# Norms of q and k by one square and one sum by head, and the transposed q and k evicted by one engine

## The chip, the cores and the metric

The kernel runs on one core of a Trainium2 chip. Its time is device time in microseconds (us). The engines are TensorE (PE in the profile's rows, with its weight loads as PEld), VectorE (DVE), ScalarE (ACT), GpSimd (POOL) and SyncE (SP), which issues most DMAs. Each works through its own queue in order and waits for the others by semaphores. Before the change the kernel took 1407.88 us, the median of three runs (1403.77 to 1408.54).

## The reference, cut to what matters

One layer of a decoder is computed for a prompt of 1024 tokens and for 8 sample sequences of 8 tokens, 1088 tokens in all. The part that the change touches is the projection with its norms by head:

```python
def rms_norm(x, w):
    x32 = x.astype(F32)
    y = x32 * lax.rsqrt(jnp.mean(jnp.square(x32), axis=-1, keepdims=True) + EPS)
    return y.astype(x.dtype) * w

p = jnp.einsum('btd,de->bte', rms_norm(x, ln1), w_in)
a, q, k, v, g_a, g_b = jnp.split(p, IN_SPLITS, axis=-1)
heads = lambda t: t.reshape(B, T, N_HEADS, HEAD_DIM)      # 12 heads of 64
return a, rms_norm(heads(q), q_norm), rms_norm(heads(k), k_norm), heads(v), g_a, g_b
```

The 12 heads are three groups of four, with window and dilation (128, 1), (512, 4) and (2048, 16). Each group's attention is computed, the three are combined by their softmax denominators, and then come gates, an output projection and an MLP of width 4096. Everything is float32, and the normed k and v are outputs too.

## The kernel before, in words

**Matmuls.** Each operand of a large matmul is split into a high and a low part (`split`, L115: ScalarE writes the rounded copy, L116, VectorE the difference, L117), and three matmuls (`PASSES`) give one product. TensorE's order is the order of the program (`manual_schedule`). The orders of the other engines' queues are laid down at build time by the framework from a simulated timeline (`schedule_with_timeline_sim`); `behind_pe` ties an instruction to the last matmul issued, so that it isn't sorted ahead of it.

**Stages.** First comes the pooling input (to about 63 us), then the three head groups in the order 2, 1, 0 (to about 416 us), then gates, output projection and MLP, which is over two thirds of the time.

**A head group.** It has nine blocks of tokens: eight of 128 prompt tokens and block 8 with the 64 sample tokens. For blocks 1 to 5 q and k come out of one product (`js = (0, 1)`, 512 columns, a full PSUM bank) and v of another; for blocks 8, 0, 6 and 7 q, k and v are three products of 256 columns. Each product is a call of `qkv_part` (L605). It orders its parts by the place that their weights hold (`js = sorted(js, key=lambda j: wts[j])`, L613), and the three places are handed out in turn.

After a product with q or k, `qkv_part` does the norm:
- squares (L642): for each head one ScalarE activation over 64 columns, from PSUM into the tile qk, with the sum of the squares accumulated into one column of `ms`;
- GpSimd adds the epsilon term (L645) and raises to the power -1/2 (L646) into `r`;
- `scale()` (L648 to L656), put off to the next `step()`, writes qk: for each head one ScalarE copy over 64 columns with `r` as the scale (L651). For the sample block VectorE multiplies k by its norm weights afterwards (L655).

`step()` (L548) runs what was put off and lets each attention in flight take one step, so that the pieces of earlier blocks' attention lie between the products of later ones.

**Transposed q and k.** `transposed` (L663) lets TensorE turn the four 128 x 128 squares of qk into one PSUM bank (L667). ScalarE copies the two of q with the norm weights as scale (L669), VectorE copies the two of k in one instruction (L670). `attend` calls it for the 24 prompt blocks, `sample_shared_keys` for the sample blocks of groups 0 and 1.

**Attention.** `attention` (L672): scores on TensorE (L684), mask and row maximum on VectorE (L693), exponential with sum on ScalarE (L694), transposes of the weights on TensorE (L703), their copy by ScalarE (L706), and the product with v (L717). Beside it run the sample's attention: its own keys of group 2 as products on GpSimd (L851) with sums on VectorE (L864), and the shared keys of groups 1 and 0 (L897 and after), with small VectorE copies (L931, L937).

## Time and profile before

| | us |
|---|---|
| median of three runs | 1407.88 |
| the profiled execution | 1405.47 |
| its span in the profile | 1403.7 |
| pooling input ends, first q product starts | about 63 |
| head groups end, gates start | about 416 |

A row of a timeline has the start in us, the length in us, engine, line, operation, tiles written and read, shapes and count; in brackets stands how long the engine was idle before it, and what released it. A row of groups has count, busy us in total, mean ns of one, and the idle time before. A row of a line has the shortest, median and longest ns of one instruction. The table of windows has for each stretch its length and the busy time of each engine, TensorE's granted clock, the DMA share and GB/s.

### The profile page before, as it was taken

How to read it: one execution, taken by the hardware profiler on the slowest of the kernel's cores; microseconds unless marked ns; L12 is line 12 of the kernel's file. 1: busy time of each engine (PE TensorE's matmuls, PEld its weight loads, DVE VectorE, ACT ScalarE, POOL GpSimd, SP SyncE). 2: the span in 40 equal slices, each digit the busy share in tenths (PEclk: the TensorE clock that was granted, in tenths of full speed). 3: DMA queues.
4: the chain of work that ended last, by engine and by line, in shares of the span. 5: the costliest groups of instructions: out<-in, count | busy, mean ns of one | idle time of the engine just before them, and what ended most of it. 6: DMA issues, size and time to landing. Idle time of an engine off the chain costs nothing.

```text
span 1403.7 us, 29517 instructions
## 1 busy us (share of the span) xinstructions
PE 1392.2 (99%) x11101; PEld 1343.0 (96%) x11101; DVE 965.2 (69%) x1766; ACT 758.0 (54%) x1962; POOL 234.2 (17%) x330
## 2 busy tenths in 40 slices
PE   9999999999999999999999999999999999999998
PEld 8988887888999999999999999999999999999998
DVE  7788775676676767876468677766665685665565
ACT  8557755777865323563336455554555544444443
POOL 0822265466500100000000000000000000000100
PEclk9999999999999999999999999999999999999999
DMA  6322788745477777975368668856758987777674
GB/s 215 117 88 101 223 219 221 205 132 146 113 254 228 246 230 243 320 233 183 127 200 285 228 221 269 269 200 211 253 186 290 321 275 261 234 240 232 205 259 169
DMA packets 184541, 303.58 MB, mean 216 GB/s; under 512 B 26567, under 2 KB 90509, under 8 KB 182350
## 3 DMA queue, kind: packets, MB, share of 16 engines
q1 hardware_dynamic: 181326, 258.04, 57.7%
q0 software_dynamic: 3072, 43.65, 9.8%
q8 instruction: 87, 1.43, 0.4%
q14 instruction: 56, 0.46, 0.1%
HBM read 231.55 MB, written 113.73 MB: 246 GB/s over the span
## 4 chain that ended last, share of the span: by engine, by line
PE 92%; DMA 3%; DVE 1%; ACT 1%; POOL 1%; issue 1%; SPq 0%; DVEq 0%; POOLq 0%; ACTq 0%
PE pz L1292 24%; PE pd L2070 24%; PE pg L1292 12%; PE ph L200 7%; PE pqk L200 5%; PE pab L1292 5%; PE pv L200 4%; PE a L328 3%; DMA raw_qkv<-in_w_in_dram 2%; PE pq L200 1%; PE pk L200 1%; PE sg0b L684 1%; PE pog0b L717 1%; PE tpg0b L703 0%; POOL mr L646 0%
## 5 line engine op out<-in xcount | busy, mean ns | idle before, releaser
L2070 PE MATMUL pd<-places 128*128 128x272 f32 x2688 | 331.8, 287 | 0.0
L2070 PEld LDWEIGHTS pd<-places 128*128 128x128 f32 x2688 | 331.6, 188 | 0.1
L116 ACT ACTIVATE places<-raw_d 128x544 fp32r<-128x544 f32 (+1 forms) x176 | 111.1, 647 | 161.8 <-DMA raw_d<-z_d 61.3
L117 DVE TENSOR_TENSOR places<-raw_d,places 128x544 fp32r<-128x544 f32 (+1 forms) x176 | 122.6, 711 | 92.3 <-ACT places L116 90.4
L2110 POOL DMA_DIRECT2D out_kv_sample_dram<-in_cache_kv_dram x96 | 47.1, 491 | 794.0 <-ACT places L116 582.9
L1292 PE MATMUL pz<-act,places 128*128 128x280 f32 (+1 forms) x1080 | 139.4, 287 | 0.0
L1292 PEld LDWEIGHTS pz<-act,places 128*128 128x128 f32 x1080 | 135.9, 188 | 0.0
L200 PE MATMUL ph<-act,places 128*128 128x280 f32 (+1 forms) x768 | 96.6, 287 | 0.0
L200 PEld LDWEIGHTS ph<-act,places 128*128 128x128 f32 x768 | 96.0, 188 | 0.1
L1292 PE MATMUL pg<-act,places 128*128 128x264 f32 (+1 forms) x576 | 75.6, 288 | 0.0
L1292 PEld LDWEIGHTS pg<-act,places 128*128 128x128 f32 x576 | 72.6, 188 | 0.6 <-issue 0.3
L1292 PE MATMUL pz<-places,apart 128*128 128x264 f32 (+1 forms) x528 | 67.9, 287 | 0.0
L1292 PEld LDWEIGHTS pz<-places,apart 128*128 128x128 f32 x528 | 66.6, 188 | 0.0
L200 PE MATMUL pqk<-places,act 128*128 128x512 f32 x240 | 60.5, 402 | 0.0
L1292 PE MATMUL pz<-act,apart 128*128 128x264 f32 (+1 forms) x456 | 59.1, 287 | 0.0
L1292 PEld LDWEIGHTS pz<-act,apart 128*128 128x128 f32 x456 | 57.5, 188 | 0.1
L200 PEld LDWEIGHTS pqk<-places,act 128*128 128x128 f32 x240 | 44.7, 192 | 9.6
L646 POOL TENSOR_TENSOR mr<-ms,mhalf 128x4 f32<-128x4 f32 (+2 forms) x39 | 52.8, 1354 | 3.1
L851 POOL TENSOR_TENSOR pck<-pck,qs 128x256 f32<-128x256 f32 x64 | 47.4, 774 | 28.6 <-DMA pck<-in_cache_kv_dram 12.4
L200 PE MATMUL pv<-places,act 128*128 128x256 f32 x384 | 50.2, 286 | 1.5 <-DVE places L117 1.5
L328 PE MATMUL a<-act,places 128*128 128x384 f32 (+1 forms) x288 | 50.5, 333 | 0.8 <-ACT act L306 0.8
L1292 PE MATMUL pab<-ab,places 128*128 128x264 f32 (+1 forms) x384 | 50.5, 287 | 0.0
(431 smaller groups left out, 2824.9 us busy)
## 6 DMA issues: line engine op xcount, KB each, us to landing
out_kv_sample_dram<-in_cache_kv_dram POOLq DMA_DIRECT2D x72, 480.0 KB, 5.2
raw_d<-z_d SPq DMA_DIRECT2D x112, 272.0 KB
z_d<-t SPq DMA_DIRECT2D x80, 272.0 KB
raw_d<-in_w_down_dram SPq DMA_DIRECT2D x80, 256.0 KB
raw_u<-in_w_up_dram SPq DMA_DIRECT2D x64, 256.0 KB
raw_qkv<-in_w_in_dram SPq DMA_DIRECT2D x36, 256.0 KB
pck<-in_cache_kv_dram SPq DMA_DIRECT2D x32, 256.0 KB
pcv<-in_cache_kv_dram SPq DMA_DIRECT2D x32, 256.0 KB
```

The lines of the kernel that those rows point to most:

```text
L116: ins = s_.activation(dst_hi, src, AF.Copy)
L117: v_.tensor_tensor(dst_lo, src, dst_hi.bitcast(F32), op=ALU.subtract)
L200: last_mm[0] = t_.matmul(out, lhs(a, k), rhs(b, k), start=(j == 0), stop=(j == len(terms) - 1))
L328: last_mm[0] = t_.matmul(pts[m][:, :n], wt[:, a, kk, m * P:(m + 1) * P], act4[b][kk][:, :, part4(c)], start=(p == 0 and kk == 0), stop=(p ...
L646: last_norm[0] = g_.tensor_tensor(r[:n, :H], ms[:n, :H], mhalf[:n, :H], op=ALU.pow)
L684: t_.matmul(sc[e][:, hp, j * P:(j + 1) * P], qT[rows, hp, :], kT[rows, 2 + hp, :], start=True, stop=True)
L717: t_.matmul(po[e * HD:(e + 1) * HD, hp, :], vr[:, h * HD:(h + 1) * HD], pTs[e][:, hp * nk + j, :], start=(j == 0), stop=(j == nk - 1))
L851: ins = g_.tensor_tensor(out, *others, op=ALU.mult)
L1292: last_mm[0] = t_.matmul(out[c], lhs(*term), rhs(*term, c), start=(first and n == 0), stop=(n == len(terms) - 1), skip_group_check=not first)
L2070: last_mm[0] = t_.matmul(outs(chain[t], Q)[c], A[:, a, t * P:(t + 1) * P], Z[:, b, c], start=(fresh and f == 0 and n == 0), stop=(f == NG ...
L2110: ins = g_.dma_start(d, a)
```

## The change

Two functions are changed.

In `qkv_part` the squares of a whole part are one ScalarE activation, without sum, and VectorE sums them by head with one reduction. GpSimd's two instructions stay. `scale()` multiplies on VectorE, the scale spread over the 64 columns of each head: one instruction over 512 columns if the order of the parts is q, k, and otherwise one of 256 columns for each of q and k. In `transposed` the copy of k moves from VectorE to ScalarE. The flag `whole` is always true, so the loops by head run zero times.

```diff
+    def by_head(t):
+        return t.rearrange("p (h d) -> p h d", d=HD)
+
     def qkv_part(g, wts, blk, name, tiles, js, middle=None, quarter=None):
...
             H = 4 * len(js)
-            for u, j in enumerate(js):
+            whole = True
+            if whole:
+                sq = qk[:n, :N] if N == 512 else qk[:n, js[0] * 256:(js[0] + 1) * 256]
+                s_.activation(sq, pt[:n, :N], AF.Square, scale=HD ** -0.5)
+                v_.tensor_reduce(ms[:n, :H], by_head(sq), axis=AX.X, op=ALU.add)
+            for u, j in enumerate(js if not whole else []):
                 for h in range(4):
                     s_.activation(qk[:n, j * 256 + h * HD:j * 256 + (h + 1) * HD],
                                   pt[:n, u * 256 + h * HD:u * 256 + (h + 1) * HD], AF.Square,
...
             def scale():
+                if whole:
+                    runs = [(0, 0, 8)] if js == [0, 1] else [(u, j, 4) for u, j in enumerate(js)]
+                    for u, j, m in runs:
+                        behind_pe(v_.tensor_tensor(by_head(qk[:n, j * 256:j * 256 + m * HD]), by_head(pt[:n, u * 256:u * 256 + m * HD]),
+                                                   r[:n, 4 * u:4 * u + m].unsqueeze(2).to_broadcast([n, m, HD]), op=ALU.mult))
                 for u, j in enumerate(js):
-                    for h in range(4):
+                    for h in range(0 if whole else 4):
                         behind_pe(s_.activation(qk[:n, j * 256 + h * HD:j * 256 + (h + 1) * HD],
...
-        v_.tensor_copy(dst[:, 2:, :n], tp[:, 2:, :n])
+        s_.copy(dst[:, 2:, :n], tp[:, 2:, :n])
```

## The prediction, made before the changed kernel was run

> **What bounds the kernel now.** I read the page first, then the table of windows for the stretch in which the changed lines run (63 to 416 us), then TensorE's own waits, and last the queues of ScalarE, VectorE and GpSimd at the places where TensorE waits.

> ```profile
> span 1403.7 us, 29517 instructions
> ...
> PE 1392.2 (99%) x11101; PEld 1343.0 (96%) x11101; DVE 965.2 (69%) x1766; ACT 758.0 (54%) x1962; POOL 234.2 (17%) x330
> ```

> ```profile
> core 0: us, PE busy (x) PEld busy (x) DVE busy (x) ACT busy (x) POOL busy (x), PEclk, DMA share, GB/s
> 63.00:416.00 353.00, 347.86 (x2815) 301.51 (x2814) 251.56 (x682) 246.17 (x1127) 158.00 (x209) 1.00 0.58 166
> 164.00:200.00 36.00, 34.46 (x276) 29.46 (x275) 22.54 (x77) 20.70 (x114) 21.05 (x30) 1.00 0.86 240
> 266.00:300.00 34.00, 31.40 (x267) 28.52 (x266) 24.15 (x64) 28.95 (x122) 16.21 (x25) 1.00 0.47 129
> 416.00:1404.00 988.00, 983.27 (x7924) 982.34 (x7922) 665.52 (x992) 465.18 (x758) 50.69 (x100) 1.00 0.73 237
> ```

> TensorE bounds it. In the stretch of the change it is busy for 347.86 of 353 us, at clock 1.00, so only 5.14 us are idle, and nearly all of that lies in two short windows where one head group gives way to the next: 36 - 34.46 = 1.54 us and 34 - 31.40 = 2.60 us. After 416 us no changed line runs. VectorE is busy for 251.56 / 353 = 71% there and ScalarE for 246.17 / 353 = 70%, so neither bounds on average; each counts only where TensorE stands still for it. In TensorE's timeline these are the places, with the idle time and its releaser in brackets:

> ```profile
> 175.44 0.86 PE L200 MATMUL pv<-places,act 128*128 128x256 f32 x5 [1.54 <-DVE places L117]
> 207.07 0.65 PE L717 MATMUL pog1b<-pTg1b,v 128*64 128x128 f32 x6 [0.42 <-ACT pTg1b L706]
> 221.90 0.71 PE L684 MATMUL sg1b<-qkTg1b 64*128 64x128 f32 x6 [0.57 <-ACT pTg1b L706]
> 270.25 0.65 PE L717 MATMUL pog1b<-pTg1b,v 128*64 128x128 f32 x6 [1.62 <-ACT pTg1b L706]
> 297.58 0.65 PE L717 MATMUL pog1b<-pTg1b,v 128*64 128x128 f32 x6 [0.98 <-ACT pTg1b L706]
> ```

> They add up to 1.54 + 0.42 + 0.57 + 1.62 + 0.98 = 5.13 us, the whole idle time. Four wait for ScalarE's copy of the transposed weights (L706), one for VectorE's part of a weight split (L117). That sum is all the change can win by ending waits. It can be a little more, since a matmul's run-through counts as busy: I estimate 0.2 us per place, 1 us in all, 6.1 us as the end of the scale. 0.5% of 1407.88 is 7.0 us, about what a measurement of this kernel can tell from no change.

> **The change, part by part.** The profiled execution took 1405.47 us (span 1403.7 and 1.8 around it), 2.41 below the median of 1407.88 and inside the runs' 1403.77 to 1408.54. I make the sum against 1405.47 and add the 2.41 at the end.

> The counts come from GpSimd's power (L646), one for each normed part:

> ```profile
> L646 POOL TENSOR_TENSOR mr<-ms,mhalf x39: 1001/1159/2000, 67.3 to 379.4; 128x4 f32<-128x4 f32 x18, 128x8 f32<-128x8 f32 x15, 64x4 f32<-64x4 f32 x6
> ```

> So 15 parts have q and k together (8 heads) and 24 have four heads. ScalarE's price for the eight-head parts:

> ```profile
> L651 ACT ACTIVATE qk<-pqk,mr 128x64 f32<-128x64 f32 x120 | 26.2, 333 | 12.9 <-POOL mr L646 12.7
> L642 ACT ACTIVATE qk<-pqk 128x64 f32<-128x64 f32 x120 | 24.7, 232 | 8.8 <-PE pqk L200 5.9 <-DMA out_kv_sample_dram<-qk 2.8
> ```

> That is 24.7 / 15 = 1.65 us of squares and 26.2 / 15 = 1.75 us of scalings a part; the four-head parts cost half. Removed from ScalarE: 15 x 3.40 + 24 x 1.70 = 92 us. Added to it: 39 squares of a whole part and 26 copies of the transposed k. The nearest rows are L706's copies from PSUM: two of 512 columns in 1.12 us (0.56 each), one of 256 in 0.42:

> ```profile
> 205.00 1.75 ACT L651 ACTIVATE qk<-pqk,mr 128x64 f32<-128x64 f32 x8 [1.90 <-POOL mr L646]
> 206.59 0.42 ACT L706 COPY pTg1b<-tpg1b 128x256 f32<-128x256 f32 x1
> ...
> 219.62 1.75 ACT L651 ACTIVATE qk<-pqk,mr 128x64 f32<-128x64 f32 x8 [3.22 <-POOL mr L646]
> 221.21 1.12 ACT L706 COPY pTg1b<-tpg1b 128x512 f32<-128x512 f32 x2
> ...
> 268.47 0.94 ACT L651 ACTIVATE qk<-pk,mr 128x64 f32<-128x64 f32 x4
> ...
> 269.77 0.43 ACT L706 COPY pTg1b<-tpg1b 128x256 f32<-128x256 f32 x1
> ...
> 295.36 0.93 ACT L651 ACTIVATE qk<-pk,mr 128x64 f32<-128x64 f32 x4 [1.18 <-POOL mr L646]
> ...
> 297.15 0.38 ACT L706 COPY pTg1b<-tpg1b 128x256 f32<-128x256 f32 x1
> ```

> Added: 15 x 0.56 + 24 x 0.42 + 26 x 0.42 = 29 us, so ScalarE loses about 63 of 246 us. At each of the four places scalings of q or k stand just ahead of the copy that TensorE needs, so this is where the relief shows.

> VectorE gains 39 sums by head and the scalings, and loses 26 copies. "One scaling per part" isn't what the code gives. The three weight places are handed out in turn, q gets place 2 and k place 0 in every group, so the sorted order is k before q; the condition that asks for q before k is never met, and an eight-head part takes two scalings of 256 columns: 15 x 2 + 24 = 54. Their nearest row is the copy from PSUM that goes (0.43 for 256 columns); for the sum it is L869:

> ```profile
> 171.75 0.43 DVE L857 SCALAR_TENSOR_TENSOR qs<-wq,qs 128x256 f32<-128x256 f32 x1 [3.11 <-PE pk L200]
> ...
> 173.00 0.43 DVE L670 COPY qkTg2b<-tqg2b 128x256 f32<-128x256 f32 x1
> ...
> 174.51 0.87 DVE L117 TENSOR_TENSOR places<-raw_qkv,places 128x512 fp32r<-128x512 f32 x1
> 175.31 0.41 DVE L869 TENSOR_REDUCE sc<-ss 128x4 f32<-128x256 f32 x1
> ```

> ```profile
> L864 DVE TENSOR_REDUCE sc<-pck x16: 1206/1220/1223, 176.7 to 278.3; 128x16 f32<-128x1024 f32 x16
> ```

> A sum over 512 columns lies between 0.41 (256) and 1.22 (1024); by the straight line it is 0.68. Together: 15 x 0.68 + 24 x 0.41 + 54 x 0.43 - 26 x 0.43 = 32 us, which takes VectorE from 252 to 284 of 353 us, 80%. It stays under TensorE, so the average costs nothing; what hides it is VectorE's idle time of 101 us.

> GpSimd's ops stay, but a wait moves. The scaling waits for GpSimd's power; so far ScalarE waited, now VectorE does, with its weight splits (L117), score masks (L693), key sums (L864) and small copies queued behind, and TensorE behind those. In exchange VectorE no longer waits for ScalarE before its transposed copy:

> ```profile
> ACT qk L651 <- POOL mr L646: 17.3, 13, 3.7
> ...
> DVE qkTg1b L670 <- ACT qkTg1b L669: 7.7, 6, 1.9
> ```

> (total us, times, longest.) Up to 17.3 us of waiting come, 7.7 go. Does TensorE see it? That depends on the lead with which a softmax tile is ready before its transposes. Two exponentials and the transposes that read them, first in the middle of a group, then at a boundary:

> ```profile
> 336.90 0.50 ACT L694 ACTIVATE smg0b<-smg0b,md 128x256 f32<-128x256 f32 x1
> ...
> 196.84 0.39 ACT L694 ACTIVATE smg1b<-smg1b,sta 128x128 f32<-128x128 f32 x1
> ```

> ```profile
> 344.27 0.66 PE L703 MATMUL tpg0b<-cst,smg0b 128*128 128x128 f32 x4
> ...
> 198.19 0.44 PE L703 MATMUL tpg1b<-cst,smg1b 128*128 128x128 f32 x2
> ```

> The lead is 344.27 - 337.40 = 6.9 us in the middle and 198.19 - 197.23 = 1.0 us at the boundary. The first covers a sum, two scalings and the longest wait (0.68 + 0.86 + 3.7 = 5.2 us); the second doesn't.

> Now the places in turn. At 207.07 and 221.90 eight scalings leave ScalarE's queue ahead of a copy whose input is there: -0.42 and -0.57 (bounds: all, or nothing if VectorE is late with the tile). At 270.25 four scalings (0.94) go, and four squares (1.65 / 2 = 0.82) become one of 0.42: -0.9 and -0.4, so -1.3 of 1.62 (bounds 0 and -1.62). At 297.58 the scalings that go (0.93, after a wait of 1.18) reappear on VectorE, which makes the masks for the same exponentials: -0.4 (bounds -0.98 and +0.9). At 175.44 VectorE works without a gap from 171.75 to the split at 174.51; the copy at 173.00 goes: -0.3 (bounds -0.43 and +0.8, a sum and a scaling slipping in front). Together -3.0. For VectorE's later masks at the two boundaries I put +1.0: two new ops (0.84) and a wait of 17.3 / 13 = 1.3 make 2.1 against a lead of 1.0, so about 1 us, at one boundary of the two (bounds 0 and +9, the slower rival). Sum: 1405.47 - 3.0 + 1.0 = 1403.5; with 2.41, **1405.9 us**.

> One price is not visible as such: VectorE and GpSimd slow each other in some ops. The small copies of L937, from SBUF to SBUF, show it, while L864's sums above, run among GpSimd's products, don't (1206 to 1223):

> ```profile
> L937 DVE COPY qS<-qkn x40: 156/176/764, 184.6 to 313.0; 64x8 f32<-64x8 f32 x32, 64x32 f32<-64x32 f32 x8
> ```

> The sums are L864's kind and the scalings read their wide operand from PSUM, so I add nothing. If the 39 + 54 new ops were stretched as L937's worst (0.764 - 0.176 = 0.59 us), it would be 93 x 0.59 = 55 us, and VectorE would stand at 339 of 353.
> [...]

> **The rivals.** *Slower: VectorE's queue stands behind GpSimd.* It decides where the lead is under 2.1 us, that is at both boundaries. There some four blocks each pass with q, k and v apart; if at each of these eight the masks come later by 2.1 - 1.0 = 1.1 us, TensorE loses 9 us, less what ScalarE's first three places still win (0.42 + 0.57 + 1.3 = 2.3): 1407.88 + 9 - 2.3 = 1414.6. For it: 17.3 us of such waits exist, and VectorE's share of the window 266 to 300 is already 24.15 / 34. Against: the 7.7 us that go, and the shorter way to the power (one square of 0.56 and a sum of 0.68 against 1.65 us of squares).
> *All waits end.* ScalarE is free at all four places and VectorE's copy goes: 1407.88 - 5.1 = 1402.8, at most 1401.8.
> [...]
> *The queues are sorted anew.* ScalarE's, VectorE's, GpSimd's and SP's orders are laid down at build time by a simulated timeline, from which the real waits deviate (ScalarE's 13 waits on the power); another order can open or close a wait of 1 to 3 us anywhere, with either sign.

> **How the numbers follow.** Forecast (a few waits end, one comes): 0.58, 1403 to 1409 with the spread of the runs. All waits end: 0.14. VectorE behind GpSimd: 0.20, 1410 to 1418. Ports: 0.03. Another order with more than 6 us: 0.05, both signs. Faster by over 0.5% needs more than the whole idle time of TensorE, so only the last case and the edge of the second give it: 0.07. Slower by over 0.5% (from 1414.9) takes about half of the slower rival, the ports and some of the last: 0.16. The rest, 0.77, is the same. The range, 1401 to 1414, holds the forecast, the second case and the lower half of the slower rival, and leaves out about 0.17.

> **What would show it.** Right: the waits for L706 at the four places gone or under 0.5 us; ScalarE in 63 to 416 us near 183 us and VectorE near 284; 54 scalings of 256 columns near 0.43; VectorE's waits on the power about as many as ScalarE's were. Wrong: TensorE's idle time in that stretch above 8 us, with VectorE's masks or weight splits as releaser; or a time under 1401, which would mean that TensorE lost time in a way its idle time doesn't show.

## The result, and the profile after

The changed kernel takes 1416.66 us (median; 1415.41 to 1419.69), the kernel before on the same chip 1407.80 us (1403.77 to 1411.55). The ratio is 1.0066, with a 95% interval of 1.0049 to 1.0084: slower, by 0.66% and at least by 0.49% (I had named 0.5% as measurable), and 2.7 us above the end of my range.

The profiled execution of after took 1419.69 us, the longest of its runs, against 1405.47 for that of before: 14.2 us lie between the two traces and 8.9 between the medians. The page:

```profile
span 1417.9 us, 29038 instructions
...
PE 1397.0 (99%) x11101; PEld 1345.9 (95%) x11101; DVE 990.6 (70%) x1833; ACT 692.5 (49%) x1379; POOL 235.9 (17%) x330
```

The averages look harmless. ScalarE lost 65.5 us and 583 instructions, VectorE gained 25.4 us, GpSimd stayed. The table of windows says where the time is (columns as in the prediction; the gates now start near 429 us):

```profile
63.00:429.00 366.00, 353.34 (x2819) 305.29 (x2818) 275.79 (x750) 181.36 (x549) 160.05 (x208) 0.99 0.57 160
429.00:1417.90 988.90, 983.27 (x7923) 982.23 (x7921) 666.80 (x992) 464.89 (x758) 50.64 (x100) 1.00 0.73 237
```

Behind the head groups TensorE is busy for 983.27 us, to the hundredth as before. The stretch of the change took 13 us more, and for two reasons: TensorE is idle for 366 - 353.34 = 12.7 us where it was 5.1, and it is *busy* for 5.5 us more with the same matmuls, at a mean clock of 0.99. TensorE's waits in total (us, times, longest):

```profile
PE tps L991 <- ACT p L985: 3.4, 1, 3.4
PE sg1b L697 <- DVE keys L980: 2.9, 1, 2.9
PE pog1b L730 <- ACT pTg1b L719: 1.7, 2, 1.3
PE pqk L200 <- DVE qk L660: 1.6, 1, 1.6
PE tqg1b L680 <- DVE sta L706: 1.3, 1, 1.3
PE sg1b L697 <- DVE p L980: 1.2, 1, 1.2
```

(Lines behind the edit moved by 13: L693 is L706, L706 is L719, L967 is L980.) The copies that TensorE waited for, L719, have shrunk to 1.7 us; but there are five new waits, four of them on VectorE and the fifth, L985, one step behind it. VectorE's and ScalarE's side of it, first VectorE from 63 to 430 us, then ScalarE over the span:

```profile
DVE qk L660 <- POOL mr L654: 9.0, 11, 1.7
```

```profile
ACT smg2b L707 <- DVE sta L706: 26.1, 7, 5.0
```

The first is the wait on GpSimd's power, which ScalarE had before (17.3 us in 13 times). The second stood at 10.2 us in 6 times: ScalarE now waits for VectorE's score masks.

**The two long stalls.** The first, row by row: GpSimd, VectorE, TensorE.

```profile
219.79 2.83 POOL L864 TENSOR_TENSOR pck<-pck,qs 128x256 f32<-128x256 f32 x4 [6.25 <-DMA pck<-in_cache_kv_dram]
222.57 0.21 POOL L653 TENSOR_TENSOR ms<-ms,stats 128x8 f32<-128x8 f32 x1
222.86 1.64 POOL L654 TENSOR_TENSOR mr<-ms,mhalf 128x8 f32<-128x8 f32 x1
...
224.53 0.76 DVE L660 TENSOR_TENSOR qk<-pqk,mr 128x256 f32<-128x256 f32 x2 [1.69 <-POOL mr L654]
225.20 1.21 DVE L877 TENSOR_REDUCE sc<-pck 128x16 f32<-128x1024 f32 x1
226.33 0.65 DVE L1145 TENSOR_TENSOR kw<-qk,wrow 128x256 f32<-128x256 f32 x1
226.90 0.29 DVE L980 TENSOR_TENSOR keys<-pss,keys 128x136 f32<-128x136 f32 x1
...
223.69 0.66 PE L716 MATMUL tpg1b<-cst,smg1b 128*128 128x128 f32 x4
227.24 1.23 PE L697 MATMUL sg1b<-qkTg1b 64*128 64x128 f32 x8 [2.89 <-DVE keys L980]
228.40 2.93 PE L200 MATMUL pqk<-places,act 128*128 128x512 f32 x6
```

GpSimd ran four products for the sample's keys before it came to the power. VectorE stood in front of the scaling for 1.69 us, then did the two scalings, a key sum and `kw`, and only then the mask L980 of the sample's scores. That mask reads the PSUM bank `pss`, and the prompt's scores `sg1b` wait for it, so TensorE stood for 2.89 us. Before, VectorE did the mask at once, while ScalarE waited for the same power (its row at 219.62 stands in the prediction); VectorE came to wait only for `kw`, behind the mask:

```profile
218.89 0.29 DVE L967 TENSOR_TENSOR keys<-pss,keys 128x136 f32<-128x136 f32 x1
...
220.59 0.78 DVE L1132 TENSOR_TENSOR kw<-qk,wrow 128x256 f32<-128x256 f32 x1 [1.13 <-ACT qk L651]
```

The second stall is built in the same way. VectorE waits twice for GpSimd, for products and then for the power, and the mask comes after it; its maximum, its exponential on ScalarE and the transposes follow late:

```profile
317.98 1.98 POOL L654 TENSOR_TENSOR mr<-ms,mhalf 128x8 f32<-128x8 f32 x1
...
317.77 0.69 DVE L902 TENSOR_TENSOR pcv<-pcv 128x512 f32<-128x512 f32 x1 [2.22 <-POOL pcv L864]
319.99 0.76 DVE L660 TENSOR_TENSOR qk<-pqk,mr 128x256 f32<-128x256 f32 x2 [1.53 <-POOL mr L654]
...
321.69 0.29 DVE L980 TENSOR_TENSOR p<-pss,cst 128x136 f32<-128x136 f32 x1
...
324.45 0.33 PE L991 MATMUL tps<-cst,p 128*128 128x128 f32 x1 [3.36 <-ACT p L985]
```

**The other three new waits.** At 211 us a mask L980 again stands behind a scaling that waited 1.35 us for the power. The waits at 180 and 186 have no wait for the power ahead of them. At 180 TensorE waits for a scaling itself. Its power was done at 178.63, but VectorE came to it only at 180.08, behind a sum and the clearing of buffers that stand ahead of it in the queue:

```profile
180.08 0.40 DVE L660 TENSOR_TENSOR qk<-pk,mr 64x256 f32<-64x256 f32 x1
...
180.54 3.06 PE L200 MATMUL pqk<-places,act 128*128 128x512 f32 x12 [1.60 <-DVE qk L660]
```

At 186 a mask comes behind a key sum that waited 1.61 us for GpSimd's products. So the moved scaling costs in two ways: what stands behind it waits for its power, and it waits for whatever stands ahead of it.

**The clock behind them.** After each of the two long stalls, matmuls run at half speed for a while: the six of 512 columns at 228.40 above take 2.93 us, while twelve took 3.04 us at 220.12. The trace's record of the granted clock has half from 226.40 us for 6.83 us, full for 92.16, and half again from 325.39 for 3.41: the three lengths are 2, 27 and 1 times 3.413 us. The table of windows, cut at steps of 3.41 us, has it in the column PEclk (the number ahead of the last two):

```profile
222.87:226.28 3.41, 1.48 (x22) 0.81 (x20) 1.75 (x3) 0.58 (x1) 3.29 (x4) 1.00 1.05 265
226.28:229.70 3.42, 2.46 (x11) 2.04 (x12) 3.31 (x11) 0.00 (x0) 1.28 (x2) 0.52 0.48 138
229.70:233.11 3.41, 3.41 (x9) 2.64 (x9) 1.03 (x9) 1.65 (x8) 1.87 (x3) 0.50 1.03 302
...
321.86:325.27 3.41, 0.82 (x7) 0.74 (x8) 3.20 (x18) 2.52 (x11) 0.95 (x2) 1.00 0.58 150
325.27:328.68 3.41, 3.41 (x19) 3.41 (x18) 2.60 (x7) 2.19 (x6) 2.17 (x4) 0.52 0.74 171
```

Each of the two stalls cost its own length and then part of the work behind it. I set the matmuls of the two traces side by side, one by one in program order, and read how far after lags. The old waits that went give back 1.70 us (at 175), 0.54 (209), 0.47 (227), 0.34 (up to 280) and 0.55 (305), 3.6 in all. The new waits add 1.84 (at 180), 1.45 (186), 1.26 (211), 2.96 (227) and 3.52 (324), 11.0 in all. The slow stretches add 2.3 and 1.7, 4.0 in all. That is 11.4 of the 12.85 us by which the head groups end late; the rest is small steps, 1.0 of it before 164 us. Another 1.4 us come at 768 to 778 us of after, behind a transfer (`u` from `u_d`) that no changed line touches.

### The profile page after: what moved, and what is told of

Same layout as the page of the kernel before. It is cut to its first block, busy times and chain, and to the rows that moved or that the text cites. A ratio compares the mean times of both kernels' runs of the same rounds, so it can differ in the third digit from the quotient of the medians.

```text
span 1417.9 us, 29038 instructions
## 1 busy us (share of the span) xinstructions
PE 1397.0 (99%) x11101; PEld 1345.9 (95%) x11101; DVE 990.6 (70%) x1833; ACT 692.5 (49%) x1379; POOL 235.9 (17%) x330
## 4 chain that ended last, share of the span: by engine, by line
PE 86%; DVE 5%; DMA 4%; POOL 2%; issue 1%; ACT 1%; SPq 0%; DVEq 0%; POOLq 0%; ACTq 0%
PE pd L2083 23%; PE pz L1305 22%; PE pg L1305 12%; PE ph L200 7%; PE pab L1305 5%; PE pqk L200 4%; PE a L328 3%; PE pv L200 3%; DMA pck<-in_cache_kv_dram 2%; PE pq L200 1%; POOL pck L864 1%; PE pk L200 1%; POOL mr L654 1%; DMA u<-u_d 1%; PE pog0b L730 1%
## 5 line engine op out<-in xcount | busy, mean ns | idle before, releaser
L117 DVE TENSOR_TENSOR places<-raw_d,places 128x544 fp32r<-128x544 f32 (+1 forms) x176 | 122.7, 712 | 90.5 <-ACT places L116 88.7
L200 PE MATMUL ph<-act,places 128*128 128x280 f32 (+1 forms) x768 | 96.6, 288 | 0.0
L200 PEld LDWEIGHTS ph<-act,places 128*128 128x128 f32 x768 | 96.0, 188 | 0.1
L200 PE MATMUL pqk<-places,act 128*128 128x512 f32 x240 | 62.8, 414 | 1.6 <-DVE qk L660 1.6
L200 PEld LDWEIGHTS pqk<-places,act 128*128 128x128 f32 x240 | 46.5, 199 | 12.0 <-DVE qk L660 1.8
L864 POOL TENSOR_TENSOR pck<-pck,qs 128x256 f32<-128x256 f32 x64 | 46.7, 762 | 29.3 <-DMA pck<-in_cache_kv_dram 20.9
L328 PEld LDWEIGHTS a<-act,places 128*128 128x128 f32 x288 | 47.9, 188 | 3.5 <-ACT act L306 1.8
```

The costliest lines, as they stand in the source:

```text
L117: v_.tensor_tensor(dst_lo, src, dst_hi.bitcast(F32), op=ALU.subtract)
L200: last_mm[0] = t_.matmul(out, lhs(a, k), rhs(b, k), start=(j == 0), stop=(j == len(terms) - 1))
L328: last_mm[0] = t_.matmul(pts[m][:, :n], wt[:, a, kk, m * P:(m + 1) * P], act4[b][kk][:, :, part4(c)], start=(p == 0 and kk == 0), stop=(p ...
L864: ins = g_.tensor_tensor(out, *others, op=ALU.mult)
```

## The experiments

My theory after the result: the scaling, now in VectorE's queue, makes everything behind it wait for GpSimd, and TensorE meets it at the sample's score masks. Rivals: the work that VectorE gained (sums and scalings) makes its masks late, with or without a wait; the copies that ScalarE took over; an order of the queues that is worse by chance. Ratios are to the kernel before, timed on the same chip, with 95% intervals.

### The scaling alone

Before, with only the scaling on VectorE: squares by head with their sums on ScalarE, copy of k on VectorE.

```diff
-            if whole:
+            if False:
                 sq = qk[:n, :N] if N == 512 else qk[:n, js[0] * 256:(js[0] + 1) * 256]
...
-            for u, j in enumerate(js if not whole else []):
+            for u, j in enumerate(js):
...
-        s_.copy(dst[:, 2:, :n], tp[:, 2:, :n])
+        v_.tensor_copy(dst[:, 2:, :n], tp[:, 2:, :n])
```

> Before, with only the scalings moved: each part is scaled by VectorE (54 multiplications of 256 columns); squares by head on ScalarE and the copy of k on VectorE stay as before. Theory A (the scaling makes VectorE's queue wait for GpSimd's power, with masks and score sums behind it, and TensorE stands still long enough at one or two places for its clock to be halved): most of the loss is here, 1413 to 1420, with a stall of TensorE near 3 us in group 1 or 0 and at least one drop of the clock. Theory B (it is the work added to VectorE, whichever it is): 54 x 0.42 = 23 of the 42 us added, so about half of the loss, 1411 to 1413, and no copy taken away from it. Theory C (the sum makes the power late, the scaling only follows): 1405 to 1409. Theory D (any change sorts the queues anew, and the time moves by a few us with no pattern): anything within 1402 to 1418.

Measured: 1412.62 us, ratio 1.0040 (1.0023 to 1.0057). The time alone fits the theory of load (1411 to 1413) and lies just under that of the wait (1413 to 1420). TensorE's two longest waits in the stretch:

```profile
PE pog1b L730 <- ACT pTg1b L719: 2.4, 1, 2.4
PE pv L200 <- DVE qk L660: 2.0, 1, 2.0
```

Neither hangs on the power. The scaling that `pv` waits for had its power at 169.25. VectorE came to that scaling late, since an instruction ahead of it in the queue had waited 5.52 us for a DMA:

```profile
172.42 0.43 DVE L870 SCALAR_TENSOR_TENSOR qs<-wq,qs 128x256 f32<-128x256 f32 x1 [5.52 <-DMA wq<-in_qk_norm_dram]
...
173.68 0.41 DVE L660 TENSOR_TENSOR qk<-pq,mr 64x256 f32<-64x256 f32 x1
```

The other wait, where the kernel before waits for 1.62 us, is for ScalarE's copy L719, behind casts (L601) of 2.21 us. Behind each of the two stands a stretch at half clock (about 175 to 182 and 274 to 278 us). The scaling alone brings over half of the loss; in this execution TensorE's long waits don't come from GpSimd.

### The whole squares and sums alone

The scaling stays by head on ScalarE, the copy on VectorE.

```diff
             def scale():
-                if whole:
+                if False:
...
-                    for h in range(0 if whole else 4):
+                    for h in range(4):
...
-        s_.copy(dst[:, 2:, :n], tp[:, 2:, :n])
+        v_.tensor_copy(dst[:, 2:, :n], tp[:, 2:, :n])
```

> Before, with only the squares changed: one ScalarE square of a whole part and one VectorE sum by head (39 sums, 0.41 to 0.70 us); scalings by head on ScalarE and the copy of k on VectorE stay. Theory A: no loss, 1403 to 1409, since no instruction of VectorE waits for GpSimd; its sums wait for ScalarE's square alone. Theory B: 39 sums are 20 of the 42 us added, about half of the loss, 1411 to 1413. Theory C: the loss is here, 1413 to 1418. Theory D: as before, no pattern.

Measured: 1407.97 us, ratio 1.0003 (0.9988 to 1.0019). 39 reductions more in VectorE's queue cost nothing by themselves that the interval shows. That speaks against VectorE's load as the cause.

### The copy alone

```diff
-        v_.tensor_copy(dst[:, 2:, :n], tp[:, 2:, :n])
+        s_.copy(dst[:, 2:, :n], tp[:, 2:, :n])
```

> Before, with only the copy of the transposed k moved from VectorE to ScalarE (26 copies of 0.38 us). Theories A, B and C: no loss, 1404 to 1410; ScalarE gets 10 us more in a stretch where it is at 70%, so the four waits for its copies before the products may grow by 1 us in all, and VectorE's 7.7 us of waits for ScalarE's half of the tile go. Theory D: no pattern.

Measured: 1405.76 us, ratio 0.9995 (0.9979 to 1.0010). No difference. The profiled execution still has one long wait, on the weight split at the boundary, with a stretch at half clock behind it (about 177 to 184 us):

```profile
PE pv L200 <- DVE places L117: 2.7, 1, 2.7
```

So the boundary can go wrong without the scaling too, in one execution, without moving the median.

### The change without the scaling

```diff
             def scale():
-                if whole:
+                if False:
...
-                    for h in range(0 if whole else 4):
+                    for h in range(4):
```

> The changed kernel with only the scaling undone: whole-part squares, sums by head on VectorE, copy of k on ScalarE, but the scalings by head on ScalarE as before. Theory A: the loss goes, 1402 to 1408, and no drop of TensorE's clock; ScalarE's scalings stay in front of its copies, so the waits of before at these copies (5 us in all) stay in part. Theory B: a loss of about a quarter, 1409 to 1411 (20 us of sums less 11 us of copies). Theory C: 1412 to 1418. Theory D: no pattern.

Measured: 1406.88 us, ratio 0.9994 (0.9976 to 1.0011). With the scaling back on ScalarE the whole loss is gone; the other two parts together neither win nor lose.

### The scaling without its wait

VectorE multiplies by a constant column; GpSimd still works out the power, and nobody reads it. So q and k are not normed in this kernel.

```diff
-                                                   r[:n, 4 * u:4 * u + m].unsqueeze(2).to_broadcast([n, m, HD]), op=ALU.mult))
+                                                   mhalf[:n, 4 * u:4 * u + m].unsqueeze(2).to_broadcast([n, m, HD]), op=ALU.mult))
```

> The changed kernel, but VectorE multiplies by a constant column in place of GpSimd's power; GpSimd still computes the power from the same sums, and nobody reads it. The norm of q and k is left out of the computation. All instructions and their counts stay; only VectorE's wait for GpSimd is gone. Theory A1 (the wait for GpSimd is what costs): the loss goes, 1403 to 1409, with no stall of TensorE over 2 us in group 1. Theory A2 (VectorE's own time for 54 scalings, 23 us at a place in its queue ahead of masks and weight splits, is what costs, whatever it waits for): 1412 to 1418 as in the changed kernel. In between: 1410 to 1412, both.

Measured: 1408.24 us, ratio 1.0017 (1.0004 to 1.0029). All of VectorE's new work is there, and a quarter of the loss. The intervals of this kernel and of after don't meet, so most of the loss goes with the wait for GpSimd, a smaller part with the work or the order of the queues. The queues are laid down anew in this kernel too, so the order may have a share in both. The profiled execution (1410.24 us) still has a wait of 2.4 us for ScalarE's copy L719, which I had not expected, and a stretch at half clock behind it (about 274 to 281 us).

### The change without the sums

Squares by head on ScalarE again; scaling and copy as in the change.

```diff
-            if whole:
+            if False:
                 sq = qk[:n, :N] if N == 512 else qk[:n, js[0] * 256:(js[0] + 1) * 256]
...
-            for u, j in enumerate(js if not whole else []):
+            for u, j in enumerate(js):
```

> The changed kernel with the squares by head on ScalarE again (no sums on VectorE): scaling on VectorE and copy of k on ScalarE stay. The scaling alone cost 0.40%, the sums alone 0.03%, all three 0.66%. If the sums make the scaling's wait worse (power later, VectorE fuller), this gives 1410 to 1413 as the scaling alone. If the copy on ScalarE is what makes it worse, 1414 to 1418.

Measured: 1411.05 us, ratio 1.0043 (1.0027 to 1.0059). In the profiles VectorE waits longer for the power here than in after, 16.4 us (14 times) against 9.0, and the kernel loses no more. The total of an engine's waits says little; what counts is what stands behind them when TensorE is due.

### The change without the copy

```diff
-        s_.copy(dst[:, 2:, :n], tp[:, 2:, :n])
+        v_.tensor_copy(dst[:, 2:, :n], tp[:, 2:, :n])
```

> The changed kernel with the copy of k on VectorE again: whole-part square, sums and scaling on VectorE. If sums and scaling work against each other, 1414 to 1419. If the copy on ScalarE makes it worse, 1410 to 1413.

Measured: 1416.19 us, ratio 1.0082 (1.0066 to 1.0098); the wait at L991 has grown from 3.4 to 4.0 us, and the one for a scaling, at 180 us in after, from 1.6 to 6.4:

```profile
PE pqk L200 <- DVE qk L660: 6.4, 1, 6.4
PE tps L991 <- ACT p L985: 4.0, 1, 4.0
```

Ahead of the longer one VectorE had waited 2.10 us for a DMA; the sums that the power needs, four products on GpSimd and the power itself came behind that.

With this the eight combinations of the three parts are complete. Scaling alone +0.40%, sums alone +0.03%, copy alone -0.05%; sums and copy -0.06%, scaling and copy +0.43%, scaling and sums +0.82%, all three +0.66%. The sums cost some 0.2 to 0.4% only where the scaling is there too (the intervals behind the 0.2 overlap). A sum then stands in the queue that waits for the power, and ahead of that power; whether it costs by its length or by the order of what follows was not settled. The copy on ScalarE gives back nothing that the intervals show.

### Waits of known length in TensorE's queue

To see what a stall does to the clock I put sixteen into the kernel before, behind the head groups: every eighth call of `by_halves` waits for a VectorE reduction over 4 to 32 times 128 elements.

```diff
     def by_halves(out, terms, lhs, rhs, first=True, between=None):
 
+        calls[0] += 1
+        red = None
+        if calls[0] % 8 == 0 and calls[0] // 8 <= 2 * len(STALLS):
+            m = STALLS[(calls[0] // 8 - 1) % len(STALLS)]
+            red = v_.tensor_reduce(stats[:, 63:64], ones.unsqueeze(1).to_broadcast([P, m, P]), axis=AX.XY, op=ALU.add)
+            behind_pe(red)
...
+                if red is not None:
+                    behind_pe(last_mm[0], red)
+                    red = None
```

> The kernel before with 16 waits put into TensorE's queue after 416 us, where it never waits otherwise: at every eighth group of 24 matmuls the first one waits for a VectorE reduction that starts after the last matmul and runs 4, 8, 12, ... 32 times 128 elements (about 0.6 to 4.4 us), the row of eight gone through twice. Its result goes into an unused column. If a wait costs only its length: 16 waits of 42 to 50 us together, 1450 to 1458. If a wait over some 2 us also halves TensorE's clock for 3.4 us or a multiple, as the clock's record around the long stalls in the changed kernel suggests: a drop behind each of the longer waits (nine or ten of 16), each 1.7 to 3.4 us more, 1465 to 1490, and none behind those under 1.7 us.

Measured: 1497.01 us in a single run, 90.6 more than before and above my ranges. The waits themselves add 66.8 us when the matmuls are set against those of before; the other 24 or so come out of thirteen stretches at half clock, 72 us long in all (the mean clock of 0.976 over the span of 1495.2 us gives the same). I had expected 42 to 50 us of waits and nine or ten stretches. Two of the waits in TensorE's timeline, and the windows around them:

```profile
417.41 8.83 PE L1301 MATMUL pg<-act,places 128*128 128x264 f32 x57 [1.88 <-DVE stats L1297]
...
846.80 5.43 PE L1301 MATMUL pz<-act,places 128*128 128x264 f32 x42 [3.00 <-DVE stats L1297]
```

```profile
415.00:418.41 3.41, 1.53 (x13) 1.35 (x12) 3.41 (x7) 1.57 (x3) 0.00 (x0) 1.00 1.05 360
418.41:421.83 3.42, 3.42 (x18) 3.42 (x17) 2.58 (x5) 0.38 (x1) 0.00 (x0) 0.52 0.82 272
...
841.63:845.05 3.42, 2.17 (x18) 1.94 (x16) 2.28 (x3) 1.60 (x4) 0.00 (x0) 1.00 0.67 203
845.05:848.46 3.41, 1.66 (x14) 1.69 (x15) 2.20 (x2) 0.47 (x1) 0.00 (x0) 1.00 1.02 322
848.46:851.87 3.41, 3.41 (x30) 3.41 (x29) 0.64 (x1) 1.69 (x3) 0.00 (x0) 1.00 0.66 190
```

The wait of 1.88 us lies in one row, TensorE is idle for 55% of it, and the next row has a clock of 0.52. The wait of 3.00 us is split over two rows, with 36% and 51% idle, and the clock stays at 1.00. In this execution all thirteen stretches begin at multiples of 3.413 us from each other, the step that the trace of after gave, and ahead of each TensorE was idle, by its matmuls' records, for 55% or more of such a step; none begins behind a step with 52% or less. The half clock lasted 3.41 us or a multiple of it, up to 10.2 us.

### The scaling one step later

The change, but the scalings of the 15 eight-head parts, and the k output behind them, are put off by one more `step()`, so that the power is done when VectorE comes to them.

```diff
-            soon(scale)
+            soon(*([lambda: None] * (len(js) == 2)), scale)
...
-            behind_pe(v_.tensor_tensor(kw, qk[:, 256:], wrow, op=ALU.mult))
-            soon(lambda: (behind_pe(dma_st(dst[:, :256], kw)), behind_pe(dma_st(dst[:, 256:], vt))))
+            def keys_out():
+                behind_pe(v_.tensor_tensor(kw, qk[:, 256:], wrow, op=ALU.mult))
+            if b in (6, 7):
+                keys_out()
+            soon(lambda: ((keys_out() if b < 6 else None), behind_pe(dma_st(dst[:, :256], kw)), behind_pe(dma_st(dst[:, 256:], vt))))
```

> The changed kernel with the scaling of the 15 eight-head parts put off by one more step, half a product or 1.5 us and more (and the k output of these blocks with it), so that the power is ready when VectorE's queue comes to it. VectorE's waits for the power (9.0 us, 11 times) should fall under 3 us. Theory A1 (that wait, and what stands behind it, is the loss; without it 0.17% was left): 1407 to 1411. If holding the product's PSUM bank longer makes TensorE wait for the bank instead: 1413 to 1418, with waits of pqk or pv for the scaling.

Measured: 1408.74 us, ratio 1.0006 (0.9996 to 1.0017). VectorE still waits 8 times for the power, but 3.9 us in all (I had expected under 3) and never over 1.1, and the clock is full in the whole of its profile (mean 1.000). At the place of the first long stall:

```profile
223.87 0.29 DVE L980 TENSOR_TENSOR keys<-pss,keys 128x136 f32<-128x136 f32 x1
...
226.75 0.76 DVE L660 TENSOR_TENSOR qk<-pqk,mr 128x256 f32<-128x256 f32 x2
...
225.52 0.72 PE L697 MATMUL sg1b<-qkTg1b 64*128 64x128 f32 x8
```

The mask now stands ahead of the scaling, the scaling waits for nothing, and the scores start without a gap. The same instructions, moved in the order, take back nine tenths of the loss. The kernel is still no faster than before.

### Only the parts of eight heads, only those of four

The scaling on VectorE for one kind of part, by head on ScalarE for the other; sums and copy as in the change.

```diff
-                if whole:
+                if len(js) == 2:
...
-                    for h in range(0 if whole else 4):
+                    for h in range(0 if len(js) == 2 else 4):
```

(and with `len(js) == 1` for the other.)

> The changed kernel, but only the 15 eight-head parts (blocks 1 to 5, in the middle of a group) are scaled on VectorE; the 24 four-head parts (blocks 8, 0, 6, 7, at the boundaries) by ScalarE as before. If the loss sits at the boundaries, where the prediction put it (lead of the softmax tiles 1 us): 1405 to 1409. If it sits in the middle, where the long stalls of the changed kernel's profile are (227 and 324 us): 1412 to 1417.

> The counterpart: only the 24 four-head parts are scaled on VectorE, the 15 eight-head parts by ScalarE. Boundaries: 1412 to 1417. Middle: 1405 to 1409.

Measured: eight heads 1409.47 us, ratio 1.0015 (1.0003 to 1.0027); four heads 1413.25 us, ratio 1.0042 (1.0026 to 1.0058). The two add up to about the whole, and by the ranges that I had named they speak for the boundaries. But the split is not a price per part: the kernel with the scaling one step later has the four-head parts on VectorE too, and those not put off, and loses 0.06%. Every edit lets the queues be laid down anew at build time, and the four-head scalings stand elsewhere in each. Which of the two kinds does the harm in the change itself stays open; in its trace the two longest stalls are behind eight-head parts.

## Why the prediction was wrong

**The bound** was right: TensorE, and only in the stretch of the head groups. The 0.2 us per place for a matmul's run-through agrees with rows of before: two transposes (L703) took 0.44 us and four 0.66, so 0.11 for each and 0.22 on top.

**The counts and prices** held. The rows of the new instructions:

```profile
L660 DVE TENSOR_TENSOR qk<-pqk,mr x30: 395/416/425, 90.9 to 372.5; 128x256 f32<-128x256 f32 x30
L660 DVE TENSOR_TENSOR qk<-pq,mr x12: 404/417/425, 68.6 to 390.5; 128x256 f32<-128x256 f32 x9, 64x256 f32<-64x256 f32 x3
L660 DVE TENSOR_TENSOR qk<-pk,mr x12: 404/418/426, 73.0 to 396.4; 128x256 f32<-128x256 f32 x9, 64x256 f32<-64x256 f32 x3
...
L647 DVE TENSOR_REDUCE ms<-qk x39: 397/414/705, 64.9 to 392.5; 128x4 f32<-128x256 f32 x18, 128x8 f32<-128x512 f32 x15, 64x4 f32<-64x256 f32 x6
...
L646 ACT ACTIVATE qk<-pqk x15: 572/597/598, 83.9 to 364.4; 128x512 f32<-128x512 f32 x15
```

30 + 12 + 12 = 54 scalings of 256 columns at 0.42, sums at 0.41 to 0.70, squares of 512 columns at 0.60. ScalarE came to 181 us (183 said) and VectorE to 276 (284 said), over a stretch 13 us longer. "One scaling per part" was indeed not what the code gives.

**The chance of 0.03 for "Ports"** had VectorE as the bound, at 339 of 353 us. No run shows ports, or that they collide. The rows show this: the 25 scalings that ran beside an instruction of GpSimd for over half of their time took 0.40 to 0.43 us, the 27 with nothing of GpSimd beside them the same, and GpSimd's own time in the stretch went from 158.0 to 160.1 us. VectorE came to 276 of 366 us. That VectorE and GpSimd slow each other in some ops stands in the trace of before: the copies L937 took 0.39 to 0.76 us in 14 of the 16 cases beside GpSimd and 0.16 to 0.20 in the 24 others, and GpSimd's products L851 took 0.61 to 0.76 us with nothing of VectorE beside them, but 1.06 to 1.23 beside five of the seven weight splits (L117) that overlapped them for over 0.5 us. The copies L670, which read PSUM as the scalings do, took at most 0.43 us with GpSimd beside them or without.

**The waits that end** were right in sum, 3.6 us measured against 3.0, but not in their parts. The split at 175 gave 1.70 instead of 0.3, the copy at 270 gave 0.34 instead of 1.3. And the gain at 175 lived for 5 us: at 180 the next product waits 1.6 us for a scaling, L660, that has yet to free its PSUM bank.

**The step that failed** is "+1.0 for VectorE's later masks at the two boundaries", with the sentence under it that the lead of 6.9 us in the middle of a group covers a sum, two scalings and the longest wait. The trace of after shows 11.0 us in its place. 3.3 lie at the first boundary, none at the second, and 7.7 in the middle, where I had counted nothing. I had measured the lead on one path, from the exponential to the transposes of the prompt's softmax. VectorE's queue has other readers with less lead: the sample's masks (L980), which free the PSUM bank that the next scores need, and the scaling itself, which frees the bank of the next product. One lead out of several isn't a cover; the shortest one decides.

Nor was 6.9 us typical of the path that I had read: before the transposes at 216.27 us it was 3.45 (an exponential at 212.33, 0.49 long), and of the 24 prompt blocks only eight have over 5.2 us for their first tile. I had also asked only what stands behind the scaling, and not what stands ahead of it: the wait at 180 is of that kind. The sign that I had named for being wrong, over 8 us of idle time with VectorE's masks as releaser, came: 12.7 us.

**What was missing** is the clock. I priced each stall at its own length. Behind two of the five new ones, 2.89 and 3.36 us long, the granted clock was 0.50, and the slower work cost 4.0 us in the profiled execution. How much of the 8.9 us between the medians is clock isn't fixed. The two runs of after at a mean clock of 0.999 and 0.998 took 1415.7 and 1415.6 us; 43 runs of the kernel before at these clocks, over three chips, have a median of 1406.7. That is 9 us at the same clock, and runs at 0.997 and 0.996 are 6 to 9 us apart, so I estimate that most of the loss is the stalls. A kernel in which the stalls stay and the drops of the clock are taken away was not tried.

**The rival** "VectorE's queue stands behind GpSimd" was the true mechanism for the larger part: 7.7 of the 11.0 us stand behind a wait for the power, 3.3 behind other things in VectorE's queue. I gave it 0.20. Its places were wrong, since I had put it at eight blocks of the boundaries, so that its 1414.6 us lie near the 1416.66 is luck. The scaling without its wait (+0.17%), the scaling put off (+0.06%) and the scaling undone (-0.06%) speak for it and against the load of VectorE and the copies. The rival "the queues are sorted anew" is not out: another order is how the same scalings come to cost 0.06% or 0.42%. As chance alone it doesn't fit: the four kernels with every scaling on VectorE and none put off, and with its wait, lose 0.40 to 0.82%, and the three with none there lose nothing that their intervals show.

**What the change could win** I had right: nothing measurable. With the scaling put off and with the constant column ScalarE has its whole relief, and neither kernel is faster than before.

## What to carry to other kernels

When an instruction that waits for a slow engine is moved to another in-order queue, the length of the instruction matters little; list everything behind it in the new queue with its reader, PSUM banks to be freed too, and take the shortest lead of them all. List also what stands ahead of it there and what that waits for. Then either move the waiting instruction back in the order until what it waits for is done, or leave it on the engine whose queue nobody is waiting for. And price a stall of TensorE with the slow work that may follow it: the shortest one with a stretch at half clock behind it was 1.61 us in these runs.

## What the runs showed of the hardware

In other profiles the idle share of the 3.413 us ahead of a drop is 60% and 72% in after (the rows of its table, cut 0.12 us earlier, give 57% and 76%), 57% and 77% with the scaling alone, 77% with the copy alone, 56% without the wait, 56% and 60% without the sums, over 89% without the copy. Three more profiles give other shares. With the scaling one step later the clock stayed at full behind a step with 54 to 55% idle (a wait of 2.09 us). With only the eight-head parts scaled on VectorE it fell after about 50% (a wait of 1.69 us), and with only the four-head parts scaled there after 47% (a wait of 1.61 us):

```profile
273.20:276.62 3.42, 1.81 (x15) 1.27 (x14) 3.42 (x9) 2.87 (x6) 2.41 (x4) 1.00 1.07 254
276.62:280.03 3.41, 3.41 (x18) 3.41 (x17) 3.02 (x10) 3.38 (x12) 0.74 (x1) 0.50 0.36 76
```

So drops came behind 47% and 50%, and none behind 52% and 54 to 55%: these records, in which the ends of matmuls are modelled, don't fix a share at which the clock falls.

The clock may bear on the scatter between the runs of one kernel. In the kernel before, over three chips, 18 runs with a mean clock of 1.000 have a median of 1405.9 us and five with 0.996 one of 1411.5; but a single run at 0.999 took 1415.6, so the clock isn't all of the scatter. Why one run of a kernel has a lower mean clock than another was not shown.
